# Two buffers for the negated blocks, and block sums spread evenly over the attention of a gated pooling and forgetting-attention block

## The chip, the cores and the metric

One core of one Trainium2 chip runs the whole kernel. The metric is device time in microseconds (us), the median of several runs of the same program. The engines are called as in the profile: PE is TensorE (its weight loads are PEld), ACT is ScalarE, DVE is VectorE, POOL is GpSimd, SP is SyncE, which here only issues transfers. Each engine works through its own queue of instructions.

## The reference

One layer, batch 1, 1024 tokens behind 16 learned tokens, width 1024, eight heads of 64:

```python
h = rmsnorm(x, norm_g)
proj = jnp.einsum('bld,dn->bln', h, w_in)
u_pool, z_pool, q, k, v, z_attn, f_logit, g_pool, g_attn = jnp.split(proj, _split_points(), axis=-1)
y_pool = causal_multiscale_pool(u_pool, pool_w, pool_scale) * jax.nn.silu(z_pool)
...
log_f = jax.nn.log_sigmoid((f_logit + b_forget).astype(jnp.float32))
y_attn = forgetting_attention(q, k, v, log_f).reshape(B, L, ATTN_WIDTH) * jax.nn.silu(z_attn)
merged = (jax.nn.sigmoid(g_pool) * jnp.einsum('blc,cd->bld', y_pool, w_up_pool)
          + jax.nn.sigmoid(g_attn) * jnp.einsum('blc,cd->bld', y_attn, w_up_attn))
return x + jnp.einsum('bld,de->ble', merged, w_out)
```

A final RMSNorm follows, and the learned tokens are dropped. The attention is causal softmax attention whose logits get the sum of the log forget gates between key and query.

## The kernel before

All products are done in three parts for precision: each operand is split into a high half (`hh`, `whi`) and a low half (`hl`, `wlo`), and high x high, high x low and low x high are added up in PSUM. The kernel has four phases:

- **Norm and first projections.** The rows of `x` are normed and transposed into `hh` and `hl`, which stay in SBUF.
- **Attention with filling.** There are sixteen units, one for each head and half of the queries. Unit i+1's scores (`ps`, L682 and L683) run between unit i's exponentials and its products with the values (`po`, L744). Between these PE is given projection work (`pj`, L170), pulled in pieces by a generator whose prices are fixed in the code. PE's order is exactly the order of the program text. The other engines' orders are made by the framework's scheduler, with hints: `after` asks for a place in an engine's order, `behind` makes a real wait.
- **Block products.** The gates `za` and `zp` (two outputs of the input projection) are not projected directly. h and the weights are cut into 2 x 2 blocks of 512, and seven products of sums of blocks, instead of eight products of blocks, are formed (L977). The output projection is done the same way (L1236).
- **Merge, output projection, final norm.**

The sums of blocks are formed in DRAM, during the attention, by adding transfers. This is the part that is changed:

- `put(dst, src)` (L586) is a copy issued by SP, placed after the latest store of projected rows.
- `add(dst, src)` (L590) is a transfer issued by POOL that adds its source to its target in DRAM. It waits for `trs[-1]`, a transpose (`mt`, L701) in the middle of the current unit, and for the copies that it reads.
- `put_h(n)` copies the high and the low half of one block of h out of SBUF, 1 MB each.
- `put_neg(blk, k, *dsts)` makes the k-th quarter of a negated block: a copy with scale -1 on ACT (L604), two subtractions of the low half on POOL (L606), then one copy of 256 KB to each target (`hsX` and `hsA` for block "21", `hsC` for block "12"). Its tile `neg` lies in a pool that has one buffer for each name unless told otherwise:

```python
t = ap_.tile([128, 512], F32, name="neg")
after(nc.scalar.activation(t, hblock(hh4, blk)[:, k], AF.Copy, scale=-1.0), exps[-1])
```

- `SUMS` tells which of these each unit does; `sums_of(i)` runs unit i's list in its order, from a hook in the middle of the next unit's maxima (`sums_at`). Where `i % 4 == 1` and i is over 1, an adding transfer for the attention's output (`add_y`) follows.

`GS` are sums of the gate weights' blocks, `TD` of the output weights', `HS` of h's. Other names that matter: `raw` is a loaded weight chunk (L151), split by ACT into `whi` (L156) and by POOL into `wlo` (L158), each with two buffers; `st` are projected rows on their way to DRAM (two buffers; evacuated by ACT at L342 and L352, stored by SP at L343 and L354); `S` are scores copied out of PSUM by ACT (L691); `graw` are weight blocks for the block products (L943), split into `gw` by ACT (L957) and POOL (L136).

Of the kernel before, what the change touches and what calls it, by code (L numbers as in the profile page):

```python
# [8 lines left out]
F32 = mybir.dt.float32  # L9
F32R = mybir.dt.float32r  # L10
# [35 lines left out]
def r32(ap):  # L46
    return ap.bitcast(F32)
# [7 lines left out]
def tile_hybrid_block(ctx, tc, x, meta, norm_g, w_in, b_forget, pool_w, pool_scale,  # L55
# [24 lines left out]
    A = ExitStack()  # L80
    ap_ = A.enter_context(tc.tile_pool(name="ap", bufs=1))
# [30 lines left out]
    def after(ins, prev):  # L112
        tc.add_manual_dep(ins.ins, prev.ins.name,
                          mybir.DependencyInfo(mybir.DependencyClass.NoSync, mybir.DependencyReason.DATA),
                          reason="order")
# [285 lines left out]

    SM = ExitStack()
    SM.enter_context(tc.manual_schedule())
    onesr = ap_.tile([128, 128], F32R, name="onesr", tag="m")
    nc.vector.memset(r32(onesr), 1.0)
    grow = gp.tile([1, D], F32, name="grow", tag="g")
    nc.scalar.dma_start(grow, norm_g)
# [156 lines left out]
    for p in range(4):  # L564
        for n in ("y", "y2"):
            spill[n, p] = dr.tile([128, SEQ], F32, name=f"sp_{n}{p}")

    TD = {n: dr.tile([512, 512], F32, name=f"td{n}") for n in (1, 2, 3, 4, 5)}
    WB = {"11": w_out[0][:512, :512], "12": w_out[0][:512, 512:], "21": w_out[0][512:, :512], "22": w_out[0][512:, 512:]}

    GS = {n: dr.tile([512, 512], F32, name=f"gs{n}") for n in (1, 2, 3, 4, 5)}
    GB = {f"{r + 1}{c + 1}": w_in[0][512 * r:512 * r + 512, col:col + 512]
          for r in range(2) for c, col in enumerate((COL_ZA, COL_Z))}
    HS = {n: dr.tile([512, 512], F32, name=f"hs{n}") for n in ("11", "22", "l11", "l22", "A", "B", "C", "X")}
# [3 lines left out]
    def hblock(d, blk):  # L578
        r, c = int(blk[0]) - 1, int(blk[1]) - 1
        return r32(d[c][:, :, 512 * r:512 * r + 512])  # L580
# [4 lines left out]
    def put(dst, src):  # L585
        after(nc.sync.dma_start(dst, src), stores[-1])  # L586
# [8 lines left out]
        put(rows_of(HS[n]), hblock(hh4, n))  # L595
        put(rows_of(HS["l" + n]), hblock(hl4, n))

    def puts(T, B):
        put(T[1], B["11"])
        put(T[5], B["12"])  # L600

    def put_neg(blk, k, *dsts):
        t = ap_.tile([128, 512], F32, name="neg")
        after(nc.scalar.activation(t, hblock(hh4, blk)[:, k], AF.Copy, scale=-1.0), exps[-1])  # L604
        for c in range(0, 512, 256):
            sub = nc.gpsimd.tensor_tensor(t[:, c:c + 256], t[:, c:c + 256], hblock(hl4, blk)[:, k, c:c + 256],  # L606
                                          op=ALU.subtract)
            after(sub, accs[-1])
        for d in dsts:
            put(HS[d][128 * k:128 * k + 128], t)  # L610

    def n21(k):
        put_neg("21", k, "X", "A")

    def n12(k):
        put_neg("12", k, "C")

    def add_y(p):
# [1 line left out]
        behind(nc.gpsimd.dma_start(d, r, accum_op=ALU.add, max_dma_last_dim=8192), trs[-1])  # L620

    SUMS = {
        0: [(n21, 0), (put_h, "11")],
        1: [(n21, 1), (add, HS["11"], HS["l11"]), (put, GS[1], GB["11"]), (put, GS[5], GB["12"])],
        2: [(n21, 2), (add, GS[1], GS[5]), (put_h, "22")],
        3: [(n21, 3), (add, HS["22"], HS["l22"]), (put, GS[3], GB["22"])],
        4: [(add, HS["X"], HS["11"]), (put, TD[1], WB["11"]), (put, TD[5], WB["12"])],
        5: [(n12, 0), (add, HS["A"], HS["22"]), (put, TD[3], WB["22"])],
        6: [(n12, 1), (add, TD[1], TD[5]), (put, HS["B"], HS["A"]), (put, GS[2], GB["11"])],
        7: [(n12, 2), (add, TD[3], TD[5]), (put, TD[2], WB["11"])],  # L630
        8: [(n12, 3), (add, HS["B"], HS["11"])],
        9: [(add, GS[3], GS[5]), (put, GS[4], GB["21"])],
        10: [(add, HS["C"], HS["B"]), (put, TD[4], WB["21"])],
        11: [(add, GS[2], GS[3])],
        12: [(add, TD[2], TD[3])],
        13: [(add, GS[4], GS[2])],
        14: [(add, TD[4], TD[2])],
    }

    def sums_of(i):  # L640
# [715 lines left out]
```

## Time and profile before

| | |
|---|---|
| median of 3 runs | 734.77 us (734.14 to 736.23) |
| the profiled execution | 734.6 us, of which 732.9 us are the span of the trace |
| mean granted TensorE clock | 0.992 of full speed |
| instructions | 10,808 |
| attention with filling | some 75 to 480 us |
| block products of the gates | 481 to 560 us |
| output projection | 650 us to the end |
| bytes moved by DMA | 119.40 MB, mean 163 GB/s |

The span is the time between the first and the last instruction of the profiled execution, and all times within the trace count from its start. In a row of the timeline the first number is the start, the second the length, and a bracket at the end tells how long the engine stood idle before and what ended that. In a list of waits the columns are the total, the number of times and the longest, all in us. SP's rows show the issuing of a transfer and not its flight.

### The profile page before, as it was taken

The page shows a single profiled execution, that of the slowest core. Times are in us where ns is not written, and L with a number is a line of the kernel's source. Part 1 is how long each engine was busy: PE and PEld are TensorE (multiplying, and loading weights), DVE is VectorE, ACT ScalarE, POOL GpSimd, SP SyncE. Part 2 cuts the span into 40 slices and gives each one's busy share as a digit, 9 for nine tenths or more (in the row PEclk, how much of TensorE's full clock was granted, in tenths as well). Part 3 has the DMA queues.
Part 4 walks back from the last instruction along what each step waited for, and adds up shares of the span by engine and source line. Part 5 has one row for each costly group of instructions (what it writes and reads, how often), then busy time and mean ns, then how long its engine had stood idle before and what let it go on. Part 6 is the DMA issues. An engine that isn't in the chain of part 4 may idle for free.

```text
span 732.9 us, 10808 instructions
## 1 busy us (share of the span) xinstructions
PE 714.6 (98%) x3637; PEld 615.7 (84%) x3637; DVE 506.5 (69%) x913; ACT 422.1 (58%) x930; POOL 326.9 (45%) x409
## 2 busy tenths in 40 slices
PE   8999999979999999999999999999999999999996
PEld 6997999978888897898988878888888888888885
DVE  5743677647789676786876758855778654887775
ACT  7653577438676675686765577242765523526445
POOL 5412337538537485255553757563643010006143
PEclk9999999989999999999999999999999999999998
DMA  9211135894992897728575498485905367672006
GB/s 304 63 30 30 30 86 189 217 322 95 233 253 69 210 245 207 194 63 196 122 160 121 118 240 222 143 285 155 332 17 193 124 205 268 223 262 62 0 2 230
DMA packets 88506, 119.40 MB, mean 163 GB/s; under 512 B 11297, under 2 KB 54305, under 8 KB 86450
## 3 DMA queue, kind: packets, MB, share of 16 engines
q1 hardware_dynamic: 84896, 99.83, 42.5%
q0 software_dynamic: 2256, 16.25, 12.7%
q10 hardware_dynamic: 1298, 2.63, 1.0%
q8 instruction: 28, 0.46, 0.3%
q14 instruction: 28, 0.23, 0.1%
HBM read 92.81 MB, written 53.67 MB: 200 GB/s over the span
## 4 chain that ended last, share of the span: by engine, by line
PE 83%; DMA 3%; ACT 3%; DVE 2%; issue 1%; POOL 1%; SPq 0%; POOLq 0%; ACTq 0%; DVEq 0%
PE pj L170 51%; PE pj L1236 8%; PE pj L977 8%; PE po L744 5%; PE pt L977 3%; PE pt L1236 2%; PE ps L683 2%; PE ps L682 2%; PE pj L515 1%; DMA hsA<-neg 1%; DMA hsC<-neg 1%; DMA graw<-in_w_in_dram 1%; POOL acc L736 1%; ACT S L691 1%; DMA raw<-in_w_in_dram 1%
## 5 line engine op out<-in xcount | busy, mean ns | idle before, releaser
L170 PE MATMUL pj<-hh,whi 128*128 128x512 f32 (+3 forms) x640 | 145.9, 355 | 0.0
L170 PE MATMUL pj<-hh,wlo 128*128 128x512 f32 (+3 forms) x640 | 143.2, 350 | 0.0
L170 PE MATMUL pj<-hl,whi 128*128 128x512 f32 (+3 forms) x640 | 142.4, 352 | 0.0
L158 POOL TENSOR_TENSOR wlo<-raw,whi 128x256 fp32r<-128x256 f32 x116 | 88.8, 815 | 75.4 <-PE pj L170 25.2
L170 PEld LDWEIGHTS pj<-hh,whi 128*128 128x128 f32 x640 | 109.1, 190 | 11.8 <-ACT hh L223 0.2
L170 PEld LDWEIGHTS pj<-hl,whi 128*128 128x128 f32 x640 | 108.8, 189 | 12.0
L170 PEld LDWEIGHTS pj<-hh,wlo 128*128 128x128 f32 x640 | 108.1, 189 | 11.4
L728 DVE TENSOR_TENSOR pl<-S,ph 128x512 fp32r<-128x512 f32 (+4 forms) x112 | 83.9, 759 | 26.2 <-ACT ph L727 25.5
L696 DVE TENSOR_TENSOR pt<-pt,S 128x400 f32<-128x400 f32 (+2 forms) x96 | 46.7, 487 | 50.3 <-ACT S L691 48.7
L736 POOL TENSOR_TENSOR acc<-acc,S 128x272 f32<-128x272 f32 (+4 forms) x80 | 74.7, 933 | 14.3 <-ACT S L724 9.0
L691 ACT ACTIVATE S<-ps,negc 128x400 f32<-128x400 f32 (+2 forms) x96 | 48.6, 514 | 39.1 <-DVE S L689 34.9
L136 POOL TENSOR_TENSOR gw<-graw,gw 128x256 fp32r<-128x256 f32 x40 | 43.4, 1117 | 36.2 <-ACT gw L957 36.2
L727 ACT ACTIVATE ph<-S 128x512 fp32r<-128x512 f32 (+4 forms) x112 | 52.7, 479 | 9.8 <-PE po L744 9.3
L724 ACT ACTIVATE S<-S 128x512 f32<-128x512 f32 (+4 forms) x112 | 49.7, 478 | 13.2 <-DVE S L723 13.0
L723 DVE TENSOR_TENSOR S<-S,pt 128x512 f32<-128x512 f32 (+4 forms) x112 | 50.7, 497 | 0.6
L682 PE MATMUL ps<-qa,ka 128*128 128x512 f32 (+4 forms) x112 | 36.9, 329 | 9.1 <-ACT S L691 9.1
L977 PE MATMUL pj<-gh,gw 128*128 128x512 f32 x180 | 42.0, 390 | 0.0
L1129 DVE TENSOR_TENSOR rl<-pj,rl 128x512 f32<-128x512 f32 x32 | 22.0, 690 | 28.6 <-PE pj L170 28.2
L156 ACT ACTIVATE whi<-raw 128x512 fp32r<-128x512 f32 x58 | 33.8, 621 | 11.6 <-DMA raw<-in_w_in_dram 5.4
L977 PEld LDWEIGHTS pj<-gh,gw 128*128 128x128 f32 x180 | 33.8, 188 | 7.1
L683 PE MATMUL ps<-ql,ka 128*128 128x512 f32 (+4 forms) x112 | 37.8, 338 | 0.0
L744 PE MATMUL po<-pl,V 128*128 128x512 f32 (+4 forms) x112 | 37.4, 334 | 0.0
(229 smaller groups left out, 1303.9 us busy)
## 6 DMA issues: line engine op xcount, KB each, us to landing
raw<-in_w_in_dram SPq DMA_DIRECT2D x31, 512.0 KB, 5.2
gs<-in_w_in_dram SPq DMA_DIRECT2D x5, 1024.0 KB, 10.7
td<-in_w_out_dram SPq DMA_DIRECT2D x5, 1024.0 KB, 8.9
xt<-in_x_dram SPq DMA_DIRECT2D x8, 512.0 KB, 6.6
gs<-gs POOLq DMA_DIRECT2D x4, 1024.0 KB, 8.7
sp_gp<-st SPq DMA_DIRECT2D x16, 256.0 KB, 4.6
td<-td POOLq DMA_DIRECT2D x4, 1024.0 KB, 9.2
sp_ga<-st SPq DMA_DIRECT2D x16, 256.0 KB, 4.2
```

What stands on the lines that cost most here:

```text
L158: ins = nc.gpsimd.tensor_tensor(lo[:, k:k + 2], raw[:, k:k + 2], r32(hi[:, k:k + 2]), op=ALU.subtract)
L170: nc.tensor.matmul(ps, a, b, start=(i == 0), stop=(i == len(seq) - 1))
L682: nc.tensor.matmul(ps[:kb, c0:], ka[:, k0:k0 + kb], qa[:, q0 + c0:q0 + 512], start=True, stop=False)
L683: nc.tensor.matmul(ps[:kb, c0:], ka[:, k0:k0 + kb], ql[:, q0 + c0:q0 + 512], start=False, stop=True)
L691: nc.scalar.activation(s[:kb, f0:], ps[:kb, f0:], AF.Identity, bias=nb_)
L723: nc.vector.tensor_tensor(s[:kb, c0:], s[:kb, c0:], self.pm[:kb, c0:], op=ALU.subtract)
L727: nc.scalar.activation(ph[:kb, c0:], s[:kb, c0:], AF.Copy)
L728: dves.append(nc.vector.tensor_tensor(pl[:kb, c0:], s[:kb, c0:], r32(ph[:kb, c0:]), op=ALU.subtract))
L736: accs.append(nc.gpsimd.tensor_tensor(acc[:kb, c0:], acc[:kb, c0:], s[:kb, c0:], op=ALU.add))
L744: nc.tensor.matmul(self.po[:, c0:], v, r[:kb, c0:], start=(b == 0 and i == 0), stop=(b == self.nb - 1 and i == 1))
L977: nc.tensor.matmul(ps, op_w[n][p][k // 2][:, k % 2, i * 128:(i + 1) * 128], op_h[n][q][k // 2][:, k % 2], start=start and m == 0, stop=m = ...
L1236: nc.tensor.matmul(ps, pick(A_, k, p)[:, i * 128:(i + 1) * 128], pick(B_, k, q)[:, c0:c1], start=start and n == 0, stop=n == 11, skip_grou ...
```

## The change

Three edits:

1. `neg` gets two buffers. The tile `onesr`, a block of ones for the warm-up products at the head of the kernel, takes one of the same two slots instead of a slot of its own; the pool grows by 1.5 KB per partition.
2. The list of copies and adding transfers is laid out anew over units 0 to 14. The set of copies, additions and negated blocks is the same. The quarters of block "21" move from units 0 to 3 to units 1 to 4; those of "12" stay in units 5 to 8. In units 1 and 3 to 8 the adding transfer stands ahead of the negated block in the list (unit 2 has no adding transfer). No unit has more than one copy of a weight block, where some had two. The adding transfer of unit 13 moves to unit 14, which now has two, and that of unit 12 moves to unit 13.
3. A helper that nothing calls is removed.

```diff
-    onesr = ap_.tile([128, 128], F32R, name="onesr", tag="m")
+    onesr = ap_.tile([128, 128], F32R, name="onesr", tag="neg", bufs=2)
...
-        t = ap_.tile([128, 512], F32, name="neg")
+        t = ap_.tile([128, 512], F32, name="neg", bufs=2)
...
-        0: [(n21, 0), (put_h, "11")],
-        1: [(n21, 1), (add, HS["11"], HS["l11"]), (put, GS[1], GB["11"]), (put, GS[5], GB["12"])],
-        2: [(n21, 2), (add, GS[1], GS[5]), (put_h, "22")],
-        3: [(n21, 3), (add, HS["22"], HS["l22"]), (put, GS[3], GB["22"])],
-        4: [(add, HS["X"], HS["11"]), (put, TD[1], WB["11"]), (put, TD[5], WB["12"])],
-        5: [(n12, 0), (add, HS["A"], HS["22"]), (put, TD[3], WB["22"])],
-        6: [(n12, 1), (add, TD[1], TD[5]), (put, HS["B"], HS["A"]), (put, GS[2], GB["11"])],
-        7: [(n12, 2), (add, TD[3], TD[5]), (put, TD[2], WB["11"])],
-        8: [(n12, 3), (add, HS["B"], HS["11"])],
-        9: [(add, GS[3], GS[5]), (put, GS[4], GB["21"])],
-        10: [(add, HS["C"], HS["B"]), (put, TD[4], WB["21"])],
-        11: [(add, GS[2], GS[3])],
-        12: [(add, TD[2], TD[3])],
-        13: [(add, GS[4], GS[2])],
-        14: [(add, TD[4], TD[2])],
+        0: [(put_h, "11")],
+        1: [(add, HS["11"], HS["l11"]), (n21, 0), (put, GS[1], GB["11"])],
+        2: [(n21, 1), (put, GS[5], GB["12"])],
+        3: [(add, GS[1], GS[5]), (n21, 2), (put_h, "22")],
+        4: [(add, HS["22"], HS["l22"]), (n21, 3), (put, GS[3], GB["22"])],
+        5: [(add, GS[3], GS[5]), (n12, 0), (put, TD[1], WB["11"])],
+        6: [(add, HS["X"], HS["11"]), (n12, 1), (put, TD[5], WB["12"])],
+        7: [(add, HS["A"], HS["22"]), (n12, 2), (put, TD[3], WB["22"])],
+        8: [(add, TD[1], TD[5]), (n12, 3), (put, HS["B"], HS["A"])],
+        9: [(add, HS["B"], HS["11"]), (put, GS[2], GB["11"])],
+        10: [(add, TD[3], TD[5]), (put, TD[2], WB["11"])],
+        11: [(add, HS["C"], HS["B"]), (put, GS[4], GB["21"])],
+        12: [(add, GS[2], GS[3]), (put, TD[4], WB["21"])],
+        13: [(add, TD[2], TD[3])],
+        14: [(add, GS[4], GS[2]), (add, TD[4], TD[2])],
```

More of the change, by code (lines that the diff above doesn't have):

```diff
@@ L596, in put_h @@
         put(rows_of(HS["l" + n]), hblock(hl4, n))
-    def puts(T, B):
-        put(T[1], B["11"])
-        put(T[5], B["12"])
     def put_neg(blk, k, *dsts):
-        t = ap_.tile([128, 512], F32, name="neg")
+        t = ap_.tile([128, 512], F32, name="neg", bufs=2)
         after(nc.scalar.activation(t, hblock(hh4, blk)[:, k], AF.Copy, scale=-1.0), exps[-1])
```

## The prediction

> **What bounds the kernel now.** I read the page first (busy shares, the clock in 40 slices, the chain that ended last), then the waits of PE alone, then busy time and clock in short stretches, then the tile that the change touches, and last the timeline around the two places where it shows.
>
> ```profile
> PE 714.6 (98%) x3637; PEld 615.7 (84%) x3637; DVE 506.5 (69%) x913; ACT 422.1 (58%) x930; POOL 326.9 (45%) x409
> PEclk9999999989999999999999999999999999999998
> ...
> PE pj L170 51%; PE pj L1236 8%; PE pj L977 8%; PE po L744 5%; PE pt L977 3%; PE pt L1236 2%; PE ps L683 2%; PE ps L682 2%; PE pj L515 1%; DMA hsA<-neg 1%; DMA hsC<-neg 1%; DMA graw<-in_w_in_dram 1%; POOL acc L736 1%; ACT S L691 1%; DMA raw<-in_w_in_dram 1%
> ```
>
> PE is busy for 98% of the span and holds nearly all of the chain. The only transfers with one per cent of it are a negated block stored to hsA, one stored to hsC and two loads of weights. One of the forty clock digits inside the kernel is an 8. So I look for the few places where PE stands. Its waits within the attention (75 to 480 us; columns: in total, times, longest) come first, then those of 430 to 440 us alone:
>
> ```profile
> PE ps L682 <- ACT S L691: 9.1, 8, 5.5
> ...
> PE ps L682 <- ACT S L691: 1.4, 1, 1.4
> ```
>
> ```profile
> core 0: us, PE busy (x), PEclk, DMA share, GB/s
> 145.00:150.00 5.00, 0.87 (x5) 0.81 1.07 354
> 150.00:155.00 5.00, 3.65 (x11) 0.51 1.03 313
> ...
> 290.00:295.00 5.00, 4.00 (x17) 1.00 1.10 370
> ...
> 435.00:440.00 5.00, 3.57 (x16) 1.00 0.84 272
> ...
> 175.00:290.00 115.00, 114.45 (x584) 1.00 0.73 188
> ...
> 300.00:430.00 130.00, 129.71 (x655) 1.00 0.61 144
> ```
>
> All of PE's 9.1 us of waiting ends with a score copy S of ScalarE, and 5.5 us of it is one wait. Outside those places PE is busy for 114.45 of 115 us and 129.71 of 130: there is no slack there into which a saved wait could sink, so what PE stops losing at one place comes off the end. PE's order is written out by hand and its work is unchanged.
>
> Why S is late, by the negated-block tile `neg` (duration min/median/max in ns, then the idle time before its instructions) and by the timeline:
>
> ```profile
> L606 POOL TENSOR_TENSOR neg<-neg,hl x16: 725/739/1067, 100.5 to 292.5; 128x256 f32<-128x256 f32 x16
> L604 ACT ACTIVATE neg<-hh x8: 617/626/641, 99.8 to 291.1; 128x512 f32<-128x512 f32 x8
> ...
>   DMA hsA<-neg: 4.5, 1
>   DMA hsC<-neg: 2.2, 1
> ...
> DMA to landing us min/median/max: 2.2/4.6/7.8
> ```
>
> ```profile
> 109.99 0.46 SPq L586 DMA_DIRECT2D hsA<-neg  x1
> ...
> 141.49 0.49 SPq L586 DMA_DIRECT2D hsA<-neg  x1
> ...
> 143.93 0.60 ACT L694 ACTIVATE pt<-S 128x512 f32<-128x512 f32 x1
> 145.17 0.70 PE L170 MATMUL pj<-hh,whi 128*128 128x384 f32 x3
> 149.05 0.63 ACT L604 ACTIVATE neg<-hh 128x512 f32<-128x512 f32 x1 [4.52 <-DMA hsA<-neg]
> 149.59 1.13 ACT L156 ACTIVATE whi<-raw 128x512 fp32r<-128x512 f32 x2
> 150.63 0.67 ACT L691 ACTIVATE S<-ps,negc 128x512 f32<-128x512 f32 x1
> 151.34 0.79 PE L682 MATMUL ps<-qa,ka 128*128 128x512 f32 x1 [5.47 <-ACT S L691]
> ...
> 291.09 0.63 ACT L604 ACTIVATE neg<-hh 128x512 f32<-128x512 f32 x1 [2.16 <-DMA hsC<-neg]
> 292.35 0.50 PE L682 MATMUL ps<-qa,ka 128*128 128x512 f32 x1 [0.71 <-ACT S L691]
> 294.07 0.51 PE L682 MATMUL ps<-qa,ka 128*128 128x512 f32 x1 [0.29 <-ACT S L691]
> ```
>
> The third negated block (149.05) has to wait until the second has left the only buffer. That one was handed to SP late, at 141.49, and landed some 7.5 us later, beside 2 MB of block copies in the same unit. ScalarE is held for 4.52 us at the head of its queue; behind it stand two halves of a weight split and the S copy for which PE needs a score bank. The seventh block does the same for 2.16 us at 291.
>
> **The change, part by part.**
>
> *Two buffers.* The third copy now needs the buffer of the first, whose transfer was issued at 109.99 and, by the slowest landing of this tile (7.8 us), was done by 117.8. ScalarE is free at 143.93 + 0.60 = 144.53, which leaves 26.7 us; the shift by a unit moves all three blocks alike. Both waits of ScalarE, 4.52 and 2.16 us, go.
>
> For PE: it stands from 151.34 - 5.47 = 145.87. If ScalarE keeps its order (negated block, two weight pieces, S), all of it moves 4.52 us earlier and PE resumes at 146.82: 0.95 us of the wait stays, and the S copy is what is late next. If the scheduler puts the negated block elsewhere, nothing stays. The gain is 4.52 to 5.47; I take 4.52, since only this order is in the trace. At 291 PE lost 0.71 + 0.29 = 1.00 us against 2.16 us of ScalarE's wait: all of the 1.00 goes.
>
> *The clock behind the long wait.* From 150 to 155 us PE was busy for 3.65 us at a mean clock of 0.51, so it lost (1 - 0.51) x 3.65 = 1.79 us of full-speed work. With 0.95 us left of the wait it should not: the waits of 1.4 us (435 to 440) and 0.71 us (290 to 295) stand beside a clock of 1.00. The sum does not hang on the following. The Trainium skill, "TensorE: Matmul & The Clock Gate", section "What's actually happening", says that the clock falls to half after at least one idle window of about 3.4 us and comes back after a busy one; by that rule alone one cold window costs an estimated 1.7 us, and a 0.95 us wait nothing. The trace agrees in both.
>
> Sum so far: 4.52 + 1.79 + 1.00 = 7.31 us.
>
> *The moved copies and adding transfers.* Their number is the same: eight negated blocks (0.63 us of ScalarE and two subtractions of 0.74 us on GpSimd each), fourteen adding transfers on GpSimd's queue, 27 copies on SP's. By unit, the copies before were 2.5, 2.5, 2.5, 1.5, 2, 1.25, 2.25 MB and so on (a negated block of rows "21" is 0.5, a block of h with its low part 2, any other 1); after they are 2, 1.5, 1.5, 2.5, 1.5, then 1.25 four times and 1 four times. In the unit of the long wait 1.5 MB goes where 2.5 went. That can only help the weight loads; I count nothing for it, with the rest of PE's waits, 9.1 - 5.5 - 1.0 = 2.6 us, as the most it could bring.
>
> What the adding transfers can hold up:
>
> ```profile
> 162.94 0.83 POOL L590 DMA_DIRECT2D gs<-gs  x1 [7.00 <-DMA hsl<-hl]
> ...
> 445.09 0.84 POOL L590 DMA_DIRECT2D td<-td  x1
> ...
> DMA to landing us min/median/max: 8.2/9.2/13.0
> ...
> L943 SPq DMA_DIRECT2D graw<-gs x8: 365/402/461, 439.2 to 519.0; - x8
> ```
>
> An adding transfer whose source was copied a unit earlier can hold GpSimd for 7.00 us, as at 162.94. Behind it stand the low halves of the weights, and PE never waited for those: its list names ScalarE alone. Before, four came one unit behind their last source (units 1 to 4), now five do (1, 3, 4, 5 and 9). Of the four only one held GpSimd for long, so the fifth costs nothing while the cover, the weights' second buffer, holds; without it, up to 7 us.
>
> Unit 14 now has two adding transfers instead of one, from about 445 us. At the slowest landing and one after the other they end 26 us later, at 471. The one new reader, the last load of a sum of the gate weights, is issued near 519, and the other sum is needed later still. What they meet on the way is the load for the second block product:
>
> ```profile
> 463.91 0.38 SPq L943 DMA_DIRECT2D graw<-in_w_in_dram  x1
> ...
> 476.25 6.12 POOL L136 TENSOR_TENSOR gw<-graw,gw 128x256 fp32r<-128x256 f32 x4 [0.64 <-ACT gw L957]
> ...
> 491.66 1.07 PE L977 MATMUL pj<-hh,gw 128*128 128x512 f32 x4
> ```
>
> Its split ends at 482.37 and PE takes it up at 491.66, so 9.3 us of delay are covered: cost 0, and 0 to 3 us if the load came 12 us late. The sum that is read first (439.2) moves from unit 11 to 12:
>
> ```profile
> 397.00 0.81 POOL L590 DMA_DIRECT2D td<-td  x1 [9.12 <-DVE mt L701]
> ```
>
> This is unit 12's adding transfer of before; 397.0 + 13.0 = 410 is 29 us ahead of the reader.
>
> *The tile layout.* The attention's pool grows by 1.5 KB per partition and the ones tile shares the first slot; its readers are the warm-up products at the head. Every tile behind is shifted, and so is what the next phase's pool waits for. The same 9.3 us cover the first of those; cost 0.
>
> Total: 734.6 (the profiled execution: 732.9 of span and 1.7 around it) - 7.3 = **727.3 us**. The median of the runs, 734.77, is 0.2 above that execution.
>
> **The rivals.**
>
> *R1, the gain is half returned.* The burst moves rather than goes: the 2 MB copy of the second diagonal block is now in unit 3 with a negated block, and a load of weights or a store comes late there. For it: ScalarE's queue is in order, and such a load does hold it:
>
> ```profile
> 435.09 1.06 ACT L825 ACTIVATE gw<-graw 128x1024 fp32r<-128x1024 f32 x1 [2.65 <-DMA graw<-in_w_in_dram]
> ```
>
> There 2.65 us of ScalarE cost PE 1.4. Two such would give 727.3 + 2.8 = 730.1 us. Against it: in the stretch from 175 to 290 us at the DMA share of 0.73 PE lost almost nothing.
>
> *R2, the change doesn't do what it says.* Something else holds the same S copy, for example the weight pieces ahead of it, and the wait only changes its name: about 734 us. Against it: those pieces ran directly after the negated block, with no gap of their own.
>
> *R3, slower.* In units 1 and 3 to 8 the adding transfer is now listed ahead of the negated block. If GpSimd takes them in that order, the subtraction waits for the landing of the adding transfer's source, and the block's copy holds SP, behind which stand the stores of projected rows, which have two buffers:
>
> ```profile
> 182.13 0.60 ACT L342 ACTIVATE st<-pj 128x512 f32<-128x512 f32 x1 [0.23 <-PE pj L170]
> 189.87 0.60 ACT L342 ACTIVATE st<-pj 128x512 f32<-128x512 f32 x1 [0.26 <-PE po L744]
> 196.60 0.58 ACT L342 ACTIVATE st<-pj 128x512 f32<-128x512 f32 x1
> ```
>
> A store buffer comes round every 7 us or so. A hold of 7.00 + 2 x 0.74 = 8.5 us overruns that by 1.5; in all seven units 10.5 us, which gives 727.3 + 10.5 = 738 us. It decides from a hold of about 7 us per unit. The Trainium skill, "TensorE: Matmul & The Clock Gate", section "Architectural detail: the array is 16× 32×32, not 1× 128×128", speaks for it: ScalarE, VectorE and GpSimd each work strictly first in, first out. The 4.52 us at 149.05 agree for ScalarE. Against R3: GpSimd's order is the scheduler's and need not be the listed one, and mostly the source has landed long before.
>
> *R4, better.* ScalarE's order changes so that nothing of the long wait stays, and lighter traffic removes the other waits too: 734.6 - 5.47 - 1.79 - 1.00 - 2.6 = 723.7 us.
>
> **How the numbers follow.** Forecast 0.64, R1 0.15, R2 0.11, R3 0.06, R4 0.04. A run of this kernel can tell about 0.3%, 2.2 us, from no change. Forecast, R4 and nearly all of R1 are faster: 0.82; R2 and a trace of R1 the same: 0.12; R3 slower: 0.06. From R4's end to somewhat beyond R1, 724.0 to 731.5 us, holds 0.83.
>
> **What would show it.** No wait of ScalarE's negated block for hsA or hsC; PE's waits in the attention down from 9.1 us to 2.5 to 4; no stretch at half clock; PE at L977 beginning some 7 us earlier. Wrong if PE's list names a weight half or a longer wait for S, if SP's queue waits for the subtraction, or if the block products begin with a gap.

## The result, and the profile after

The changed kernel takes 726.99 us (median; 726.48 to 727.94). The kernel before, run beside it, takes 735.49 (734.14 to 736.23). The ratio is 0.9888, with an interval of 0.9868 to 0.9908: 8.5 us or 1.1% faster. In the changed kernel all lines behind `puts` stand four lower: the negated block is made at L600 and L602, `S` is copied at L687, the scores run at L678 and L679, the block products at L973.

From the page after: the span, busy time by engine, the granted clock in 40 slices, the chain by engine and by line.

```profile
span 725.5 us, 10804 instructions
...
PE 712.8 (98%) x3637; PEld 613.8 (85%) x3637; DVE 506.9 (70%) x913; ACT 422.4 (58%) x930; POOL 330.8 (46%) x409
...
PEclk9999999999999999999999999999999999999998
...
PE 84%; ACT 3%; DVE 2%; DMA 1%; POOL 1%; issue 1%; POOLq 0%; ACTq 0%; DVEq 0%
PE pj L170 53%; PE pj L1232 8%; PE pj L973 8%; PE po L740 5%; PE pt L973 3%; PE pt L1232 2%; PE ps L679 2%; PE ps L678 2%; PE pj L515 1%; DMA graw<-in_w_in_dram 1%; POOL acc L732 1%; ACT S L687 1%; DMA raw<-in_w_in_dram 1%; ACT S L720 1%; PE pj L300 0%
```

The span is 7.4 us shorter (732.9 before). The 8 inside the row of clock digits is gone (the last digit is an 8 in both), and so are the two stores of negated blocks from the chain.

PE's waits within the attention (75 to 475 us; in total, times, longest), then PE's busy time and clock in the stretches that answer to those of before:

```profile
PE ps L678 <- ACT S L687: 3.2, 6, 1.3
```

```profile
145.00:150.00 5.00, 4.32 (x23) 1.00 1.04 381
150.00:155.00 5.00, 5.00 (x32) 1.00 0.99 313
...
175.00:290.00 115.00, 114.45 (x583) 1.00 0.75 199
300.00:420.00 120.00, 119.70 (x605) 1.00 0.66 160
425.00:430.00 5.00, 3.71 (x17) 1.00 1.08 367
```

The DMA engines are as full at 145 to 155 us as before (shares of 1.04 and 0.99, before 1.07 and 1.03). PE no longer feels it: 4.32 us of work instead of 0.87, then 5.00 at full clock instead of 3.65 at 0.51. The small stop at 425 to 430 us is the one that stood at 435 to 440.

The tile `neg` (it has no list of idle time any more, only durations and landings), and the timeline around the place:

```profile
L602 POOL TENSOR_TENSOR neg<-neg,hl x16: 730/744/1067, 129.5 to 284.8; 128x256 f32<-128x256 f32 x16
L600 ACT ACTIVATE neg<-hh x8: 616/620/635, 123.1 to 283.2; 128x512 f32<-128x512 f32 x8
...
DMA to landing us min/median/max: 2.4/7.1/8.6
```

```profile
129.49 1.69 POOL L602 TENSOR_TENSOR neg<-neg,hl 128x256 f32<-128x256 f32 x2
...
136.23 1.09 POOL L590 DMA_DIRECT2D hs<-hsl  x1
...
141.93 0.42 SPq L586 DMA_DIRECT2D hsA<-neg  x1
143.28 0.62 ACT L600 ACTIVATE neg<-hh 128x512 f32<-128x512 f32 x1
146.45 0.67 ACT L687 ACTIVATE S<-ps,negc 128x512 f32<-128x512 f32 x1
147.17 0.50 PE L678 MATMUL ps<-qa,ka 128*128 128x512 f32 x1 [0.69 <-ACT S L687]
...
473.27 1.08 PE L973 MATMUL pj<-hh,gw 128*128 128x512 f32 x4
```

The block is still handed over at 141.93, and the landings have become slower, not faster (median 7.1 us, before 4.6). But ScalarE begins the next block at 143.28 without waiting for them, and PE's 5.47 us have shrunk to 0.69. The first block product begins at 473.27 instead of 480.65: 7.38 us, so the whole gain lies in the attention.

The account over the two profiled executions: PE waits 9.1 - 3.2 = 5.9 us less, and loses 1.79 us less to the half clock. By 42 us, ahead of the attention, it stands 0.58 us later (the same projection products begin at 42.61 instead of 42.03). That makes 7.1 of the 7.4 us.

### The profile page after: what moved, and what is told of

The parts are those of the page before. It is cut to its first block, busy times and chain, and to the rows that moved or that the text cites. A ratio compares the mean times of both kernels' runs of the same rounds, so it can differ in the third digit from the quotient of the medians.

```text
span 725.5 us, 10804 instructions
## 1 busy us (share of the span) xinstructions
PE 712.8 (98%) x3637; PEld 613.8 (85%) x3637; DVE 506.9 (70%) x913; ACT 422.4 (58%) x930; POOL 330.8 (46%) x409
## 4 chain that ended last, share of the span: by engine, by line
PE 84%; ACT 3%; DVE 2%; DMA 1%; POOL 1%; issue 1%; POOLq 0%; ACTq 0%; DVEq 0%
PE pj L170 53%; PE pj L1232 8%; PE pj L973 8%; PE po L740 5%; PE pt L973 3%; PE pt L1232 2%; PE ps L679 2%; PE ps L678 2%; PE pj L515 1%; DMA graw<-in_w_in_dram 1%; POOL acc L732 1%; ACT S L687 1%; DMA raw<-in_w_in_dram 1%; ACT S L720 1%; PE pj L300 0%
## 5 line engine op out<-in xcount | busy, mean ns | idle before, releaser
L158 POOL TENSOR_TENSOR wlo<-raw,whi 128x256 fp32r<-128x256 f32 x116 | 90.7, 826 | 84.4 <-ACT whi L156 33.1
L687 ACT ACTIVATE S<-ps,negc 128x400 f32<-128x400 f32 (+2 forms) x96 | 48.5, 514 | 37.0 <-DVE S L685 33.0
L136 POOL TENSOR_TENSOR gw<-graw,gw 128x256 fp32r<-128x256 f32 x40 | 45.5, 1173 | 29.8 <-ACT gw L953 12.2
L973 PE MATMUL pj<-gh,gw 128*128 128x512 f32 x180 | 42.0, 389 | 0.0
L973 PEld LDWEIGHTS pj<-gh,gw 128*128 128x128 f32 x180 | 33.8, 188 | 7.1
L678 PE MATMUL ps<-qa,ka 128*128 128x512 f32 (+4 forms) x112 | 36.5, 326 | 3.2 <-ACT S L687 3.2
L679 PE MATMUL ps<-ql,ka 128*128 128x512 f32 (+4 forms) x112 | 37.5, 335 | 0.0
```

What stands on the lines that cost most here:

```text
L158: ins = nc.gpsimd.tensor_tensor(lo[:, k:k + 2], raw[:, k:k + 2], r32(hi[:, k:k + 2]), op=ALU.subtract)
L678: nc.tensor.matmul(ps[:kb, c0:], ka[:, k0:k0 + kb], qa[:, q0 + c0:q0 + 512], start=True, stop=False)
L679: nc.tensor.matmul(ps[:kb, c0:], ka[:, k0:k0 + kb], ql[:, q0 + c0:q0 + 512], start=False, stop=True)
L687: nc.scalar.activation(s[:kb, f0:], ps[:kb, f0:], AF.Identity, bias=nb_)
L973: nc.tensor.matmul(ps, op_w[n][p][k // 2][:, k % 2, i * 128:(i + 1) * 128], op_h[n][q][k // 2][:, k % 2], start=start and m == 0, stop=m = ...
```

## The experiments

Theory: the gain is that of the second buffer alone, since it takes the landing of a block's copy off ScalarE's queue; the lists bring nothing. Rivals: the lists, by lighter units, do part of it; or GpSimd's order costs something that hides a larger gain. A second question came up on the way: why a copy of 256 KB took 7.5 us at all.

**One half of the change each.** `e1_buffers` is the kernel before with the first edit alone (the ones tile shares the slot in it too). `e2_lists` is the changed kernel without that edit:

```diff
 e1_buffers, against before
-    onesr = ap_.tile([128, 128], F32R, name="onesr", tag="m")
+    onesr = ap_.tile([128, 128], F32R, name="onesr", tag="neg", bufs=2)
-        t = ap_.tile([128, 512], F32, name="neg")
+        t = ap_.tile([128, 512], F32, name="neg", bufs=2)
 e2_lists, against after: the same four lines, the other way round
```

> The first edit alone: two buffers and the shared slot, with the old list of copies and adding transfers. Theory (the second buffer does all of it): ScalarE's negated block waits for no transfer, PE's waits in the attention fall from 9.1 us to 3 to 4, no half clock, 727 us (726 to 728.5), the time of the changed kernel. Rival (the spread list carries half or more, since the 2.5 MB of the second unit still fall together): PE keeps a wait of 2 us or more near 146 us, 730 us or more.

> The new list alone, with one buffer and the old layout of the pool. Theory: every quarter still needs the quarter before to have left. The second block is copied near 143 us and the first's transfer is issued at 142 and lands 4 to 8 us later, so ScalarE is held for 3 to 6 us at the same place, PE stands 4 to 6 us with half clock behind it, and another 1 to 2 us go at the fourth block (190 us) and the eighth (283 us): 733 to 737 us, no better than before by more than 1 us. Rival (lighter traffic is what matters): 730 us or less.

Measured: `e1_buffers` 726.66 us (726.13 to 727.66), ratio 0.9886 [0.9869, 0.9902], the whole gain. `e2_lists` 737.9 us (736.23 to 740.52), ratio 1.0041 [1.0027, 1.0055], so slower than before, and slower than either of its expectations. PE's waits of the one:

```profile
PE ps L682 <- ACT S L691: 3.1, 6, 1.3
```

and of the other, with the idle time before its negated blocks, its timeline and its stretches:

```profile
PE ps L678 <- ACT S L687: 10.7, 10, 5.1
```

```profile
  DMA hsA<-neg: 7.8, 2
  DMA hsC<-neg: 2.3, 1
```

```profile
148.71 0.63 ACT L600 ACTIVATE neg<-hh 128x512 f32<-128x512 f32 x1 [4.34 <-DMA hsA<-neg]
```

```profile
150.00:155.00 5.00, 3.99 (x12) 0.52 0.59 179
155.00:160.00 5.00, 5.00 (x24) 0.80 1.00 295
```

With one buffer the lists leave the long wait where it stood in time; it now stands before the second block instead of the third. ScalarE is held there for 4.34 us, though 1 MB less is copied in this unit, and two units on for another 7.8 - 4.34 = 3.5 us. PE waits 10.7 - 9.1 = 1.6 us more and loses (1 - 0.52) x 3.99 + (1 - 0.80) x 5.00 = 2.9 us to the clock, 1.1 more than before: 2.7 of the 3.1 us by which this span (736.0) is longer. The second buffer is the whole of the change's gain.

**GpSimd's order (the rival that ended slower).** In the changed kernel the subtractions run at 129.49, ahead of the adding transfer at 136.23, although they are listed behind it. `e3_sub_behind` makes them stand behind it on GpSimd:

```diff
...
+        adds.append(nc.gpsimd.dma_start(d, r, accum_op=ALU.add, max_dma_last_dim=8192))
+        behind(adds[-1], trs[-1])
...
+            after(sub, adds[-1])
```

> The changed kernel, with the subtraction of each negated block placed behind the latest adding transfer in GpSimd's order, which is the order that the prediction's slower rival needs. Rival R3 of the prediction: the copies of the blocks hold SP's queue, stores of projected rows come late, ScalarE and then PE wait; 738 us. Theory: the adding transfers wait for little beyond their transpose, SP is not held for a store buffer's 7 us, PE's list of waits stays with ScalarE's S alone: 727 us, within 1.5 us of the changed kernel.

Measured: 726.6 us (725.86 to 727.18), ratio 0.9883 [0.9865, 0.9901]; PE's waits come to 3.7 us. That order costs nothing that can be told, even where it is forced. The hold that the rival needs did not arise: GpSimd's idle time before its adding transfers ends with the transpose `mt` each time (48.8 us in ten waits), never with the landing of a source.

**The neighbours of the block's copy.** In `e7_light` (kernel before, one buffer) the two 1 MB copies of unit 1 go to units 3 and 4, and the adding transfer that needs them to unit 5:

```diff
-        1: [(n21, 1), (add, HS["11"], HS["l11"]), (put, GS[1], GB["11"]), (put, GS[5], GB["12"])],
-        2: [(n21, 2), (add, GS[1], GS[5]), (put_h, "22")],
...
+        1: [(n21, 1), (add, HS["11"], HS["l11"])],
+        2: [(n21, 2), (put_h, "22")],
...
```

> The kernel before, one buffer, with the two 1 MB copies of the second unit (sums 1 and 5 of the gate weights) moved to units 3 and 4 and their addition to unit 5. If traffic made the second block land late: it lands in some 4.6 us (the tile's median) instead of 7.5, ScalarE is held for 1.5 to 2 us instead of 4.5, PE stands about 2.5 us, and with a wait that short no half clock follows: 730 us. If the late handing over to SP at 141.5 and not the traffic is the cause: ScalarE is held for 4 us or more as before, half clock included, 734 us.

Measured: 735.25 us (732.89 to 739.26), ratio 1.0009 [0.9994, 1.0024]: no difference. ScalarE's hold falls to 3.50 us only, between the two expectations, and PE's stop to 4.5 us. (The execution of the trace took 732.89 us, 2.4 below the median, so its rows show this run at its best.) Its timeline, and what the DMA queues moved (packets, MB, share of the 16 engines' time) first in 139 to 144 us and then in 144 to 147:

```profile
147.60 0.63 ACT L604 ACTIVATE neg<-hh 128x512 f32<-128x512 f32 x1 [3.50 <-DMA hsA<-neg]
```

```profile
q0 software_dynamic: 108, 0.88, 99.5%
q1 hardware_dynamic: 59, 0.00, 1.8%
...
q1 hardware_dynamic: 763, 1.12, 99.9%
q0 software_dynamic: 16, 0.00, 0.9%
```

The block's copy was handed over at 141.09. Until 144 the queue of the adding transfers (q0) holds the engines, and SP's queue (q1) moves nothing that counts; then it moves 1.12 MB in 3 us, and the block lands at 147.5. So the adding transfer HS11 += l11, issued at 135.37, rather than the 1 MB copies, is what the block seems to stand behind. Two runs test this by taking that transfer away, the first leaving the two copies where they were:

```diff
 e10_add_away, against before
-        1: [(n21, 1), (add, HS["11"], HS["l11"]), (put, GS[1], GB["11"]), (put, GS[5], GB["12"])],
+        1: [(n21, 1), (put, GS[1], GB["11"]), (put, GS[5], GB["12"])],
-        3: [(n21, 3), (add, HS["22"], HS["l22"]), (put, GS[3], GB["22"])],
+        3: [(n21, 3), (add, HS["11"], HS["l11"]), (add, HS["22"], HS["l22"]), (put, GS[3], GB["22"])],
 e11_all_away, against e7_light: the same add moved from 1 to 3
```

> Kernel before, one buffer, old lists, and one thing moved: the adding transfer of HS11 += l11 is issued at unit 3 instead of unit 1; the two 1 MB copies stay in unit 1. Theory: the negated block's copy is handed over late (141 us) and then stands behind the adding transfer in flight, which held the DMA engines at 99.5% from 139 to 144 us in the kernel with the copies moved away. Without it the copy shares the engines with the 1 MB copies alone: it should land in 5 to 6 us (before 8.6, copies moved 6.4), ScalarE's hold fall from 4.52 to 2 to 3.5 us, TensorE's idle time there to 3 to 4 us, and the time come to 731 to 734. Rival, the late handing over alone counts and the neighbours hardly matter: the copy still takes over 6 us, 734 to 736.

> Kernel before, one buffer, and unit 1 holds nothing but the negated block: the two 1 MB copies and the adding transfer are all issued at later units. Theory (the block's copy stands behind what else is in flight): handed over at 141 us it lands in 2.2 to 4.6 us, ScalarE is held 0 to 1.6 us near 144.5, TensorE idles at most 2.5 us there, no half clock follows, and 728 to 730 remains, the 1.0 us of the wait at block 7 among it. Rival, the late handing over alone counts: the landing stays at 6 us or more, and the time at 733 or more.

Measured: `e10_add_away` 728.36 us (727.79 to 728.78), ratio 0.9895 [0.9874, 0.9916]; `e11_all_away` 729.02 us (728.81 to 729.49), ratio 0.9906 [0.9888, 0.9924]. Of `e10_add_away`: PE's waits, the queues in 139 to 144 us, the block's landing (KB, us) and the next block's start:

```profile
PE ps L682 <- ACT S L691: 4.8, 8, 1.5
```

```profile
q1 hardware_dynamic: 659, 1.12, 81.7%
...
hsA<-neg SPq DMA_DIRECT2D x1, 256.0 KB, 2.6
```

```profile
141.19 0.45 SPq L586 DMA_DIRECT2D hsA<-neg  x1
...
144.16 0.62 ACT L604 ACTIVATE neg<-hh 128x512 f32<-128x512 f32 x1
```

Handed over as late as before, the copy lands after 2.6 us, and ScalarE is not held at all. My expectation was too careful (a landing of 5 to 6 us, 731 to 734 us; the 8.6 us that it gives for the landing before should be 7.5): it let the two 1 MB copies share the engines, but they are issued behind the block's and do not disturb it, and taking them away as well gains nothing more. What is left against the second buffer is mainly the wait at the seventh block: 2.49 us of ScalarE, at 284.89, which cost PE 1.03 + 0.30 us.

**Handing the block over early.** The subtraction is done at 130.55 in the kernel before, yet SP takes the copy at 141.49, because `put` places it behind the latest store of projected rows. In `e8_early_hand` (one buffer, old lists) it has no such place:

```diff
-            put(HS[d][128 * k:128 * k + 128], t)
+            nc.sync.dma_start(HS[d][128 * k:128 * k + 128], t)
```

> The kernel before with one buffer and the old list; only the order hint of the negated blocks' copies is left out, so that SP takes the second block's copies at some 131 us, right behind the subtraction, instead of at 141. If the late handing over is what made the buffer the limit: the block has landed by 138 us, ScalarE's third block near 144 us waits for nothing, PE's waits fall below 4 us, no half clock, 727 to 729 us with one buffer. If a single buffer is too few in any case (the landing itself takes until 149): 733 us or more.

Measured: 726.62 us (725.8 to 730.38), ratio 0.9887 [0.9865, 0.9909]. Its timeline, and the landing:

```profile
130.87 0.42 SPq L610 DMA_DIRECT2D hsA<-neg  x1
...
142.63 0.62 ACT L604 ACTIVATE neg<-hh 128x512 f32<-128x512 f32 x1
...
146.52 0.50 PE L682 MATMUL ps<-qa,ka 128*128 128x512 f32 x1 [0.73 <-ACT S L691]
```

```profile
hsA<-neg SPq DMA_DIRECT2D x1, 256.0 KB, 4.3
```

One dropped hint brings what the second buffer brings, and costs no SBUF. So the long wait needed three things at once: one buffer, the late handing over, and an adding transfer in flight. Each of the three was taken away alone, and each time PE's wait of 5.5 us fell to under 1 us.

**Is the rest worth something?** `a2_after` is the changed kernel once more, as the measure for `e6_early_load` (the changed kernel with the load of the first block weights at unit 12) and `e9_both` (old lists, two buffers, the early load):

```diff
-        if i == 13:
+        if i == 12:
```

> The changed kernel again, on the chip of the next two: 726 to 728 us.

> The changed kernel with the load of the first gate-weight block issued one unit earlier (unit 12 instead of 13). It goes at what the change left: PE's longest remaining wait, 1.3 us near 427 us, behind ScalarE's 2.5 us wait for that load. Theory (the load is what is late): that wait of PE falls to 0.3 us or less, 725 to 726 us, about 1 us below the changed kernel. Rival (the two halves of the split, 1.05 us each, stand ahead of the score copies whenever the load lands): PE still waits about 1 us there, no difference that can be told.

> Two buffers with the old list, and the load of the first gate-weight block one unit earlier. If the new list brings nothing beside the second buffer, this is level with the changed kernel that has the earlier load, 725 to 726 us, whichever theory holds for that load. If the new list matters once the buffer is there, it is slower than that one by over 1 us.

Measured: `a2_after` 726.14 us (726.06 to 726.8), ratio 0.9877 [0.9854, 0.99]; `e6_early_load` 725.57 (725.53 to 725.96), 0.9867 [0.9848, 0.9887]; `e9_both` 726.02 (725.25 to 727.12), 0.9873 [0.9852, 0.9894]. In the changed kernel, at the load, and then in `e6_early_load`:

```profile
427.73 1.06 ACT L821 ACTIVATE gw<-graw 128x1024 fp32r<-128x1024 f32 x1 [2.52 <-DMA graw<-in_w_in_dram]
...
429.42 0.51 PE L678 MATMUL ps<-qa,ka 128*128 128x512 f32 x1 [1.29 <-ACT S L687]
```

```profile
426.17 0.50 PE L678 MATMUL ps<-qa,ka 128*128 128x512 f32 x1 [0.50 <-ACT S L687]
```

ScalarE's wait of 2.52 us goes, but the two pieces of the split still run ahead of the S copy that PE waits for, so 0.50 of PE's 1.29 us stay: more than the theory's 0.3, less than the rival's 1. `e6_early_load` is the fastest median of the study, 0.6 us ahead of the changed kernel; the two intervals overlap, and the difference is less than a run can tell. Without the new lists (`e9_both`) it is the same again.

## Why the prediction was right

- **The long wait: right.** Predicted 4.52 us of it gone and 0.95 left; measured 5.47 - 0.69 = 4.78 gone. The S copy was late next, as said. ScalarE takes up the block at 143.28, a little ahead of the place that was worked out.
- **The clock: right.** 1.79 us predicted; all of 150 to 155 us is at 1.00 after. That the prediction's estimate of 1.7 us for one cold window lies so close is in part luck: before, the clock stood at half for some 6.8 us, and PE idled through the first part of them. The other runs bear the reason out: PE stops of 4.5 (`e7_light`), 5.1 (`e2_lists`) and 5.5 us (before) are followed by clocks of 0.66, 0.52 and 0.51, stops of up to 1.7 us (`e3_sub_behind`) by none below 1.00. The Trainium skill, "TensorE: Matmul & The Clock Gate", section "What's actually happening", puts the limit at an idle window of about 3.4 us; the runs agree, but none has a stop between 1.7 and 4.5 us.
- **The stop at 291 us: right.** Its 1.00 us went.
- **The total: right in size.** 7.31 us predicted for the profiled execution, 7.4 measured in the span. What was not in the sum nearly cancels: 0.26 us more of the long wait and some of the small waits, against the 0.58 us by which the work ahead of the attention ends later; 0.3 of the 7.4 us is put down to nothing.
- **The moved copies and adding transfers at nothing: right beside two buffers, not by themselves.** The old lists with two buffers take as long as the new ones (726.66 and 726.99). But "that can only help" was wrong for one buffer, where the lists cost 0.4%.
- **The cause given for the late landing: wrong in part.** "Handed to SP late" holds (`e8_early_hand`). "Beside 2 MB of block copies" does not: without those copies the median is the same (`e7_light`), with them and without the adding transfer the landing takes 2.6 us (`e10_add_away`). No term of the sum hung on it, because two buffers take the landing out of the way whatever its cause.
- **The cover at the block products: the cost was 0, but the cover is nearly used up.** Before, the low halves of the second product's split ended 9.3 us ahead of PE. In the changed kernel that margin is 2.5 us (ready 8.48 us behind the first product, needed 11.01 behind it). ScalarE's half now waits for the last store of the attention's output to free its place:

```profile
471.05 1.06 ACT L953 ACTIVATE gw<-graw 128x1024 fp32r<-128x1024 f32 x1 [6.92 <-DMA sp_y<-t]
```

  In `e1_buffers` the low halves are ready at 5.47 us and in `e2_lists` at 6.28, against 1.72 before: the shifted layout and the new lists each take a part. I gave that shift no price because of the cover, and should have said that it uses it.
- **The count of close adding transfers: one short, without effect.** Five were counted one unit behind their last source. The second of unit 14 is a sixth, since it reads the sum that unit 13 forms. In the changed kernel GpSimd's idle time before adding transfers names no landing at all.
- **The rivals.** Half of the gain returned: no new wait of that kind appeared. Only a new name: no. Slower by GpSimd's order: it did not arise, and forced it costs nothing. Better: only by the further 0.26 us at the long wait.

## What to carry to other kernels

A wait at the head of an in-order engine's queue is priced by the engine that starves behind it, and by the clock it loses after that: here 4.5 us of ScalarE cost PE 5.5 + 1.8 us. When a small store lands late, look at when it was handed over and at which other queue holds the DMA engines meanwhile, before the bytes of its neighbours are counted. A second buffer, an earlier hand-over and a moved neighbour each removed the long wait alone (the moved neighbour left 1.3 us of PE's waiting at another block), so after one of them little is left there for the other two; pairs of them were not run.

## What the runs showed of the hardware

An adding transfer in DRAM can hold up the other queue for microseconds. In `e7_light`, while a block's copy stood handed over to SP (141 to 144 us; packets, MB, share of the 16 engines' time):

```profile
q0 software_dynamic: 55, 0.45, 96.3%
q1 hardware_dynamic: 55, 0.00, 2.9%
```

As soon as the adding transfer was done, SP's queue moved 1.12 MB in 3 us. The Trainium skill, "DMA: Bandwidth & Descriptors", section "Queues, rings and completion order", says that each DMA engine goes round between its queues packet by packet. These rows agree: 55 packets of the one queue stand against 55 of the other. The sharing is by packets and not by bytes: those of the adding transfer hold 0.45 MB / 55, some 8 KB each, and the view counts all 55 of SP's as under 512 bytes. A likely source of the small packets is a store of 8 KB (`sums`), handed over ahead of the block at 137.35: it took 7.7 us to land here and 2.4 us in `e10_add_away`, without the adding transfer. That the block's copy stood behind this store is a reading that no row names and no run tested. Whether the engines were really busy with the adding transfer or stood waiting in it for memory, the rows do not tell; that stays open, as does why one such transfer took 8.2 us and another 13.0.

What the clock costs does not follow the length of the stop. After 4.5 us of idling (`e7_light`) PE lost (1 - 0.66) x 5.00 = 1.7 us, after 5.1 us (`e2_lists`) 2.9, after 5.5 us (before) 1.79. It follows the work that falls into the slow stretch. In 1-us stretches the clock is at 0.50 from some 150.2 to 153.6 us in `e7_light`, 150.2 to 157.0 in `e2_lists` and 148.1 to 154.9 in the kernel before, estimates of 3.4, 6.8 and 6.8 us. PE idled through the first half of the last, until 151.34, and worked through most of the other two. Of `e7_light`:

```profile
150.00:155.00 5.00, 5.00 (x19) 0.66 0.72 253
```
